# Eleven small loads at the start of a backbone block: issued from ScalarE's queue in place of SyncE's

## The chip, the cores and the metric

One core of one Trainium2 chip runs the whole program. The metric is the device time of one execution in microseconds (us). Times of a profiled execution come with a span, from its first to its last recorded work.

## The reference, cut to what matters

One layer (DEPTH is 1) of a generator block on 1024 tokens of width 1024, all in float32. The conditioning vector c gives six modulation rows; the tokens pass a multi-scale window mean with a grouped projection, a layer norm, a SwiGLU and a second layer norm.

```
s_c = silu(c);  mod_x = s_c @ mod_w + mod_b          # 1024 x 6144
sh1, sc1, g1, sh2, sc2, g2 = split(mod_x, 6)
hx = x * (1 + sc1) + sh1
p  = [window_mean(hx, w) - hx for w in (2, 4, 8, 16)]   # 256 channels each
ox = einsum('blgc,gcd->blgd', p, pool_w) * pool_scale
x  = layer_norm(ALPHA * x + g1 * ox, ln_g[0], ln_b[0])
x  = layer_norm(ALPHA * x + g2 * swiglu(x * (1 + sc2) + sh2), ln_g[1], ln_b[1])
```

## The kernel before, in words

The tokens lie in eight row tiles of 128 tokens (512 KB each), taken in two halves of four: first the tiles 1, 2, 3, 4, then 5, 6, 7, 0. The kernel first does the pooling stage, and then two long SwiGLU stages in which TensorE (PE) is nearly always busy. This case is about the first thirty microseconds.

**The modulation.** `mod_load` brings a 512 KB piece of mod_w (tile `mw`, eight pieces for each of the six modulation rows), and `mod_add` adds it on VectorE (DVE) into an accumulator `acc`, weighted by a column of `s_col`, the silu of c (line 489 for a first piece, 491 for the others). The eight pieces of sc1 come first, then those of g1. `columns` (line 506) has PE turn an accumulator into columns, and `mod_col_done` (line 518) takes them out as `sc1`.

**The window means.** For each of eight channel tiles and each token tile, `pool_inner` (line 461) multiplies the tokens by a band matrix that lies in the tile `consts` (`cst`); `pool_outer` (line 466) then adds, for a whole half, what comes from the neighbouring tokens, out of the tile `halo` (32 rows of x) and a further part of `consts` (`halo_band`). `pool_hi` (ACT, line 471) and `pool_lo` (DVE, line 474) take the result out of PSUM. `scale_bank` (PE, line 541) spreads pool_scale, which lies in `psc`, over the partitions.

**The order.** A list written out by hand, `ORDER_OF_ISSUE`, names each job in the order in which it is issued; each engine carries out its own instructions in that order. Loads are issued by SyncE (SP) in the rows shown here, one behind the other. In the list's order the first 25 loads are: 1 `rows` (c), 2 `mw`, 3 `acc` (mod_b of g1, behind a fill of `acc` by GpSimd), 4 `consts` (band matrices of two groups), 5 `mw`, 6 `x`, 7 `mw`, 8 to 10 `rows` (mod_b, ln_g, ln_b), 11 `x`, 12 `mw`, 13 `x`, 14 `mw`, 15 `x`, 16 `mw`, 17 to 20 `halo`, 21 `consts` (with `halo_band`), 22 `consts` (the other two groups), 23 and 24 `mw`, 25 `psc`. `to_columns` transposes the `rows` on PE; its first call gives `s_col` on ScalarE (ACT, line 347).

In the list, the jobs that ACT carries out are, up to the end of the first `pool_hi`: `to_columns.0` (`s_col`), and nothing else. All eleven loads that the diff touches stand ahead of that `pool_hi`: loads 4 and 8 to 10 ahead of `to_columns.0`, loads 17 to 22 and 25 behind it.

Of the kernel before, what the change touches and what calls it, by code (L numbers as in the profile page):

```python
# [17 lines left out]
P = 128  # L18
# [11 lines left out]
REACH = 8  # L30
# [189 lines left out]
def trunk_kernel(ctx: ExitStack, tc: tile.TileContext, x, c, mod_w, mod_b, ln_g, ln_b, ffn_w_in, ffn_w_out,  # L220
                 pool_w, pool_scale, consts, out):
    nc = tc.nc
# [26 lines left out]
    def big(name, dt=F32, shape=(P, 1024)):  # L249
        return take("big", name, dt, shape)  # L250
# [7 lines left out]
    def small(name, shape, bufs=1, tag=None):  # L258
        return keep.tile(list(shape), F32, tag=tag or name, name=name, bufs=bufs)
# [31 lines left out]
    tiles = {}  # L291
# [6 lines left out]
    rows = small("rows", (72, P))  # L298
# [5 lines left out]
    cst = small("consts", (P, N_MID + N_HALO + N_EDGE + N_SUMS))  # L304
# [30 lines left out]
            nc.scalar.copy(bands["starts"][:, :, at_], src)  # L335

    def vector_rows(a, b, src):
        nc.sync.dma_start(rows[a:b, :], src.rearrange("(j p) -> j p", p=P))

    def to_columns(n):  # L340

# [12 lines left out]
        nc.sync.dma_start(xr[i], x[i * P : (i + 1) * P, :])  # L354

    def load_consts(s):
        nc.sync.dma_start(cst[:, s], consts[:, s])

    def load_halo(half):
        if half == 0:  # L360
            tiles["halo",] = big("halo", F32, (32, D))
        halo, (before, after), r = tiles["halo",], HALO_ROWS[half], 2 * REACH * half
        nc.sync.dma_start(halo[r : r + REACH, :], x[before - REACH : before, :])
        nc.sync.dma_start(halo[r + REACH : r + 2 * REACH, :], x[after : after + REACH, :])

    job(fill_ones)
    job(fill_constants)
# [6 lines left out]

    def load_scale():
        tiles["psc",] = big("psc")
        nc.sync.dma_start(tiles["psc",][0:1, :], pool_scale.rearrange("(o d) -> o d", o=1))

    def mod_start(j):

# [4 lines left out]
    def gate_load(pair, kh):  # L385
        load(("wi", pair, kh), ffn_w_in[kh * HALF : (kh + 1) * HALF, pair * 256 : (pair + 1) * 256].rearrange(
            "(k p) n -> p k n", p=P), (P, 4, 256))

    job(vector_rows, 0, 8, c[0])
    job(mod_load, SC1, 0)  # L390
    job(load_consts, slice(0, 2 * BAND))
    job(mod_load, SC1, 1)
    job(load_x, ORDER[0][0])
    job(mod_load, SC1, 2)
    for a, b, src in ((8, 56, mod_b), (56, 64, ln_g[0]), (64, 72, ln_b[0])):
        job(vector_rows, a, b, src)
# [3 lines left out]
    for half in range(2):  # L400
        job(load_halo, half)
    job(load_consts, slice(N_MID, cst.shape[1]))
    job(load_consts, slice(2 * BAND, 4 * BAND))
    for k in (6, 7):
        job(mod_load, SC1, k)
    job(mod_start, G1)
    job(load_scale)
    for k in range(KT):
        job(mod_load, G1, k)
# [999 lines left out]
```

## Time and profile before

| | us |
|---|---|
| median of 3 runs | 750.62 |
| lowest, highest | 748.63, 751.89 |
| profiled execution, its own time | 749.97 |
| its span | 748.2 |

The profiled execution has 1.77 us around its span. In the rows below, PE is TensorE, PEld its weight loads, DVE VectorE, ACT ScalarE, POOL GpSimd, SP SyncE; SPq is the queue of transfers that SyncE issues. A row's "idle before <-" says how long the engine had stood still and what ended that. PEclk is the granted clock of TensorE as a share of full speed.

### The profile page before, as it was taken

The numbers are of one execution on the slowest core, as the hardware profiler recorded it, in microseconds if no ns is written. First come the engines' busy times: TensorE is split into PE (matmuls) and PEld (weight loads), VectorE is DVE, ScalarE is ACT, GpSimd is POOL, SyncE is SP. The second block draws the span as 40 slices with busy tenths as digits, with TensorE's granted clock in tenths as the row PEclk, the third lists the DMA queues.
The fourth block names the chain that finished last, engine by engine and source line by source line (L and its number), as shares of the span: only waits on it lengthen the run. The fifth ranks groups of instructions, "written<-read, shape, count | busy, mean of one in ns | idle before, by whom it ended". The sixth has DMA issues, their size and how long they took to land.

```text
span 748.2 us, 9131 instructions
## 1 busy us (share of the span) xinstructions
PE 723.9 (97%) x3326; PEld 604.8 (81%) x3326; DVE 554.9 (74%) x675; ACT 274.1 (37%) x353; POOL 168.3 (22%) x133
## 2 busy tenths in 40 slices
PE   6988999999999999999999999999999999999994
PEld 6768988888887888888888888888888888888783
DVE  3797855517288788899998777965878679646986
ACT  0321873435983221311312212212556334336411
POOL 0000000011206546483743624600000000233100
PEclk7587999999999999999999999999999999999998
DMA  8998249674929679797987798455799856999612
GB/s 303 368 409 298 114 159 375 225 237 164 330 86 292 200 239 254 210 310 241 320 264 186 240 265 212 156 202 207 277 376 391 290 193 220 262 302 286 173 57 84
DMA packets 115346, 182.85 MB, mean 244 GB/s; under 512 B 7739, under 2 KB 66819, under 8 KB 115046
## 3 DMA queue, kind: packets, MB, share of 16 engines
q1 hardware_dynamic: 108038, 164.97, 63.8%
q0 software_dynamic: 7264, 17.30, 11.5%
q8 instruction: 26, 0.43, 0.2%
q14 instruction: 18, 0.15, 0.1%
HBM read 142.14 MB, written 51.64 MB: 259 GB/s over the span
## 4 chain that ended last, share of the span: by engine, by line
PE 84%; DVE 7%; DMA 3%; ACT 3%; issue 2%; POOL 0%; SPq 0%; POOLq 0%; DVEq 0%; ACTq 0%
PE ps_v L895 39%; PE ps_x L1106 16%; PE ps_gate L761 14%; PE ps_y L1106 8%; PE ps_col L506 2%; DVE acc L491 2%; DVE ylo L270 1%; PE ps_ox L262 1%; PE ps_ox L263 1%; PE ps_ox L264 1%; DMA x<-in_x 1%; DMA consts<-in_consts 1%; ACT h L699 1%; DMA mw<-in_mod_w 1%; DVE t L270 1%
## 5 line engine op out<-in xcount | busy, mean ns | idle before, releaser
L895 PE MATMUL ps_v<-t,w0h 128*128 128x512 f32 x352 | 109.2, 391 | 0.0
L761 PE MATMUL ps_gate<-h,wih 128*128 128x512 f32 x352 | 109.0, 391 | 0.0
L267 ACT CAST yhi<-yraw 128x1024 fp32r<-128x1024 f32 x77 | 78.4, 1051 | 81.7 <-DMA yraw<-in_ffn_w_out 23.4
L270 DVE TENSOR_TENSOR ylo<-yraw,yhi 128x1024 fp32r<-128x1024 f32 x77 | 91.6, 1218 | 20.6 <-ACT yhi L267 11.4
L962 POOL TENSOR_TENSOR s<-raw,raw 128x512 f32<-128x512 f32 x22 | 31.5, 1432 | 319.3 <-DMA raw<-in_ffn_w_in 300.5
L918 ACT ACTIVATE a<-a 128x512 f32<-128x512 f32 x22 | 13.9, 632 | 229.9 <-DVE a L917 229.9
L895 PEld LDWEIGHTS ps_v<-t,w0h 128*128 128x128 f32 x352 | 66.1, 188 | 14.6 <-issue 1.0
L761 PEld LDWEIGHTS ps_gate<-h,wih 128*128 128x128 f32 x352 | 65.7, 188 | 13.7 <-issue 0.5
L491 DVE SCALAR_TENSOR_TENSOR acc<-mw,s_col,acc 128x1024 f32<-128x1024 f32 x42 | 55.9, 1331 | 19.1 <-DMA mw<-in_mod_w 18.3
L895 PE MATMUL ps_v<-t,w0l 128*128 128x512 f32 x176 | 68.6, 390 | 1.4 <-DVE w0l L270 1.4
L761 PE MATMUL ps_gate<-h,wil 128*128 128x512 f32 x176 | 68.5, 389 | 0.0
L1106 PE MATMUL ps_x<-yhi 128*128 128x512 f32 x176 | 68.5, 389 | 0.0
L1106 PE MATMUL ps_x<-ylo,yhi 128*128 128x512 f32 x176 | 68.5, 389 | 0.0
L1106 PE MATMUL ps_x<-yhi,ylo 128*128 128x512 f32 x176 | 68.5, 389 | 0.0
L895 PE MATMUL ps_v<-t,ws 128*128 128x512 f32 x264 | 63.4, 389 | 0.0
L1068 POOL DMA_DIRECT2D yraw<-in_ffn_w_out x22 | 18.7, 853 | 195.6 <-PE ps_x L1106 163.6
L895 PEld LDWEIGHTS ps_v<-t,ws 128*128 128x128 f32 x264 | 49.5, 188 | 10.3
L895 PE MATMUL ps_v<-h,w1h 128*128 128x512 f32 x176 | 54.2, 389 | 0.0
L895 PE MATMUL ps_v<-t,w1h 128*128 128x512 f32 x176 | 54.2, 389 | 0.0
L1106 PE MATMUL ps_y<-yhi 128*128 128x512 f32 x132 | 51.4, 390 | 0.9 <-DVE yv L1352 0.9
L1106 PE MATMUL ps_y<-yhi,ylo 128*128 128x512 f32 x132 | 51.4, 389 | 0.0
L1106 PE MATMUL ps_y<-ylo,yhi 128*128 128x512 f32 x132 | 51.4, 389 | 0.0
(157 smaller groups left out, 1386.5 us busy)
## 6 DMA issues: line engine op xcount, KB each, us to landing
mw<-in_mod_w SPq DMA_DIRECT2D x48, 512.0 KB, 9.2
raw<-in_ffn_w_in SPq DMA_DIRECT2D x88, 256.0 KB, 5.2
wi<-in_ffn_w_in SPq DMA_DIRECT2D x22, 512.0 KB, 6.2
yraw<-in_ffn_w_out SPq DMA_DIRECT2D x44, 256.0 KB, 5.4
yraw<-ed SPq DMA_DIRECT2D x33, 256.0 KB, 6.0
ed<-in_ffn_w_out POOLq DMA_DIRECT2D x6, 1024.0 KB, 10.5
pd<-pk SPq DMA_DIRECT2D x11, 512.0 KB, 5.2
gd<-gk SPq DMA_DIRECT2D x11, 512.0 KB, 2.9
```

The costliest lines, as they stand in the source:

```text
L262: nc.tensor.matmul(ps, lh, rh, start=first, stop=False)
L263: nc.tensor.matmul(ps, lh, rl, start=False, stop=False)
L267: nc.scalar.copy(hi, src)
L270: nc.vector.tensor_tensor(lo, src, hi.bitcast(F32), ALU.subtract)
L491: nc.vector.scalar_tensor_tensor(acc, w, s_col[:, k : k + 1], acc, ALU.mult, ALU.add)
L506: nc.tensor.matmul(tiles["ps_col", j][:, n * WIDE : (n + 1) * WIDE], t[:, n * P : (n + 1) * P], by, start=first and n == 0, stop=last and ...
L761: nc.tensor.matmul(ps, x, y, start=k == n == 0, stop=k % 4 == 3 and n == 2, skip_group_check=k > 3)
L895: nc.tensor.matmul(ps, x, y, start=fresh and first, stop=last, skip_group_check=not fresh)
L918: nc.scalar.activation(a[:, 1], a[:, 1], ACT.Silu)
L962: nc.gpsimd.tensor_tensor(s, up1, up2, ALU.add)
L1068: nc.gpsimd.dma_start(raw[n][:, 1], ADDED[n // PAIRS](n % PAIRS), accum_op=ALU.add)
L1106: nc.tensor.matmul(ps, s[x][:, r * P : (r + 1) * P], t[y][:, d], start=fresh and j == m == 0, stop=j == PAIRS - 1 and m == 2, skip_group_c ...
```

## The change

The loads of `rows` other than that of c, all three loads of `consts`, the four of `halo` and the one of `psc` are issued by ScalarE. Their place in `ORDER_OF_ISSUE`, their sizes and their destinations stay. The loads of c, `mw`, `x` and `acc` stay with SyncE.

```
     def vector_rows(a, b, src):
-        nc.sync.dma_start(rows[a:b, :], src.rearrange("(j p) -> j p", p=P))
+        (nc.sync if a == 0 else nc.scalar).dma_start(rows[a:b, :], src.rearrange("(j p) -> j p", p=P))
...
     def load_consts(s):
-        nc.sync.dma_start(cst[:, s], consts[:, s])
+        nc.scalar.dma_start(cst[:, s], consts[:, s])
...
-        nc.sync.dma_start(halo[r : r + REACH, :], x[before - REACH : before, :])
-        nc.sync.dma_start(halo[r + REACH : r + 2 * REACH, :], x[after : after + REACH, :])
+        nc.scalar.dma_start(halo[r : r + REACH, :], x[before - REACH : before, :])
+        nc.scalar.dma_start(halo[r + REACH : r + 2 * REACH, :], x[after : after + REACH, :])
...
     def load_scale():
         tiles["psc",] = big("psc")
-        nc.sync.dma_start(tiles["psc",][0:1, :], pool_scale.rearrange("(o d) -> o d", o=1))
+        nc.scalar.dma_start(tiles["psc",][0:1, :], pool_scale.rearrange("(o d) -> o d", o=1))
```

## Rows read from the trace of the kernel before

**Rows 1.** The page: the span, and the busy time of each engine.
```profile
span 748.2 us, 9131 instructions
PE 723.9 (97%) x3326; PEld 604.8 (81%) x3326; DVE 554.9 (74%) x675; ACT 274.1 (37%) x353; POOL 168.3 (22%) x133
```

**Rows 2.** The chain of work that ended last, in order of time, of its first 140 us the pieces that the text below names: start, length (us), what.
```profile
2.27 0.25 SPq L383
2.56 0.34 SPq L357
2.94 5.38 DMA mw<-in_mod_w
8.34 6.58 DMA x<-in_x
14.94 5.50 DMA consts<-in_consts
20.57 1.85 PE ps_pt L466 x8
22.43 4.44 PE ps_pt L461 x20
26.87 1.91 PE ps_psc L541 x4
28.78 2.73 PE ps_col L506 x16
...
32.21 1.28 DVE acc L491
...
40.23 3.52 PE ps_g L548 x4
...
95.44 38.11 PE ps_gate L761 x168
```

**Rows 3.** The queue of SP in order of time: start, time of the issue (us), line, transfer.
```profile
4.36 0.61 SPq L338 DMA_DIRECT2D rows<-in_mod_b  x1
5.02 0.93 SPq L338 DMA_DIRECT2D rows<-in_ln_g  x1
5.99 0.36 SPq L338 DMA_DIRECT2D rows<-in_ln_b  x1
6.39 0.35 SPq L354 DMA_DIRECT2D x<-in_x  x1
...
8.34 0.33 SPq L354 DMA_DIRECT2D x<-in_x  x1
...
11.03 0.33 SPq L354 DMA_DIRECT2D x<-in_x  x1
...
14.94 1.75 SPq L357 DMA_DIRECT2D consts<-in_consts  x2
17.65 2.13 SPq L295 DMA_DIRECT2D mw<-in_mod_w  x2
19.82 0.29 SPq L377 DMA_DIRECT2D psc<-in_pool_scale  x1
```

**Rows 4.** What SP's queue waited for in the first 30 us: us in total, times, longest.
```profile
SPq L354 <- DMA mw<-in_mod_w: 2.9, 3, 1.1
SPq L357 <- DMA x<-in_x: 1.0, 1, 1.0
```

**Rows 5.** PE, DVE and ACT in order of time up to 32 us: start, us, engine, line, operation, operands, and in brackets the idle time before and what ended it.
```profile
17.68 2.08 PE L461 MATMUL ps_pt<-consts,x 128*128 128x129 f32 x8 [0.61 <-DMA x<-in_x]
20.57 1.85 PE L466 MATMUL ps_pt<-consts,halo 32*128 32x16 f32 x8 [0.81 <-DMA consts<-in_consts]
...
8.42 1.28 DVE L491 SCALAR_TENSOR_TENSOR acc<-mw,s_col,acc 128x1024 f32<-128x1024 f32 x1 [0.77 <-DMA mw<-in_mod_w]
11.11 1.28 DVE L491 SCALAR_TENSOR_TENSOR acc<-mw,s_col,acc 128x1024 f32<-128x1024 f32 x1 [1.41 <-DMA mw<-in_mod_w]
27.24 1.28 DVE L491 SCALAR_TENSOR_TENSOR acc<-mw,s_col,acc 128x1024 f32<-128x1024 f32 x1 [0.18 <-DMA mw<-in_mod_w]
31.53 0.17 DVE L518 SCALAR_TENSOR_TENSOR sc<-ps_col,cols 128x8 f32<-128x8 f32 x1 [3.01 <-PE ps_col L506]
...
0.74 1.28 ACT L347 ACT_TABLE_LOAD   x1 [0.74 <-PEq L1396]
6.65 0.21 ACT L347 ACTIVATE s_col<-cols 128x8 f32<-128x8 f32 x1 [4.63 <-DVE cols L345]
21.18 2.06 ACT L471 CAST pt<-ps_pt 128x512 fp32r<-128x512 f32 x4 [14.32 <-PE ps_pt L466]
```

**Rows 6.** Stretches of the start (A:B in us): length, busy time of each engine with its instructions, then the granted clock of TensorE, the share of the 16 DMA engines that was busy, and what they moved in GB/s.
```profile
core 0: us, PE busy (x) PEld busy (x) DVE busy (x) ACT busy (x) POOL busy (x), PEclk, DMA share, GB/s
4.00:6.00 2.00, 2.00 (x12) 2.00 (x11) 0.00 (x0) 0.00 (x0) 0.00 (x0) 1.00 0.77 213
10.00:18.00 8.00, 6.54 (x26) 5.71 (x27) 3.98 (x4) 0.00 (x0) 0.00 (x0) 0.50 1.02 401
22.40:26.20 3.80, 3.80 (x18) 3.80 (x18) 3.51 (x5) 2.08 (x6) 0.00 (x0) 0.50 1.00 364
26.50:29.50 3.00, 3.00 (x15) 1.62 (x14) 1.84 (x2) 1.17 (x2) 0.00 (x0) 1.00 1.02 407
29.80:31.50 1.70, 1.70 (x10) 1.70 (x10) 0.00 (x0) 0.00 (x0) 0.00 (x0) 0.50 0.99 395
```

**Rows 7.** Transfers by issuing line in the first 35 us: engine, count, size of one, median us from issue to landing.
```profile
halo<-in_x SPq DMA_DIRECT2D x4, 32.0 KB
consts<-in_consts SPq DMA_DIRECT2D x2, 144.0 KB, 4.4
consts<-in_consts SPq DMA_DIRECT2D x1, 100.0 KB, 5.5
```

**Rows 8.** Waits between 20 and 100 us, that of the accumulations for their loads: us in total, times, longest.
```profile
DVE acc L491 <- DMA mw<-in_mod_w: 2.0, 2, 1.8
```

## The prediction

> **What bounds the kernel now.** The page comes first: PE is busy for 97% of the span [rows 1]. From 95 us on the chain of work is PE at its dense SwiGLU matmuls [rows 2], so a change in the loads of the first 20 us can only move the moment at which that stretch begins. The next view is therefore the chain in order of time. Its start is three transfers in a row: a piece of mod_w (2.94, 5.38 us), a tile of x (8.34, 6.58 us), and a load of `consts` (14.94, 5.50 us), which lets PE begin `pool_outer` at 20.57 [rows 2]. From there PE runs without a break to 31.5, DVE waits for it (the accumulations from 32.21 on), and so on to the dense stretch [rows 2].
>
> Why each transfer of that chain begins as the one before lands is seen in SP's queue. The issue at 8.34 is load 13, and it waits for load 5; the issue at 14.94 is load 21, and it waits for load 13 [rows 3, 4]. So a load is held until the one eight places ahead of it in the list has landed. It is not the time of an issue (0.3 to 0.9 us [rows 3]) that spaces the later loads, but this rule and the rate of the DMA engines, which between 10 and 18 us are full: share 1.02, 401 GB/s [rows 6]. Only before that is there room: 0.77 and 213 GB/s from 4 to 6 us [rows 6].
>
> **The change part by part.** I assume that the rule of eight places goes on counting over both queues; the trace has one hardware queue only, and the last rival takes the other case.
>
> *Loads 4 and 8 to 10 leave SP.* Load 5 (`mw`) follows load 3, whose issue starts at 2.27 behind GpSimd's fill, so it can be issued at 2.56 in place of 2.94: 0.38 us earlier [rows 2]. Load 11 (`x`), issued at 6.39, no longer stands behind the three issues from 4.36 on, 2.0 us [rows 3]. What this is worth is bounded by the gap in the rate: from 4 to 6 us (401 - 213) GB/s x 2 us = 0.38 MB are not moved, which is 0.94 us at 401 GB/s. Below, it is worth nothing, if the DMA engines and not the queue made the gap: 1.5 MB (loads 5 to 7) had been issued by then and still ran at 213 GB/s. I take 0.38 us, the shift of load 5, as that load alone is on the chain.
>
> *Loads 17 to 21 go to ACT's queue.* Load 21 still waits for load 13, so it is issued no earlier than that lands, about 14.5. But in SP's queue it took 5.5 us for 100 KB [rows 7], behind the 512 KB loads issued ahead of it; on a queue of its own it has none ahead. The trace has no small load on a second queue: bounds are nothing saved (5.5 us), and the 100 KB at 401 GB/s, 0.26 us, besides a start that no row gives. The nearest small load in a shorter queue is one of the two 144 KB `consts`, whose median is 4.4 us [rows 7]. Even at 4.4 us it would land at 19.0 and be off the path, since the next thing late is PE itself: the eight matmuls of the fourth x tile run from 17.68 for 2.08 us, to 19.76 [rows 5]. So the most that the earlier `consts` alone gives is PE's wait, 0.81 us [rows 5].
>
> The Trainium skill, DMA: Bandwidth & Descriptors, section "Issuing engines are not separate DMA queues", says that loads from different engines end on the same 16 DMA engines, and that issuing from several saves only the issuing time; by that sentence `consts` lands no sooner and the sum would be nothing. Its section "Queues, rings and completion order" says that each DMA engine takes turns between the queues that have work; by that one `consts` passes the big loads. No row of before can choose, as it has one such queue.
>
> *What the small loads take from the big ones.* If they pass, the fourth x tile (load 15, issued at 11.03, landing at 17.65) has four `halo` loads and one `consts` ahead of it that used to be behind: 4 x 32 + 100 = 228 KB [rows 7], 0.58 us at 401 GB/s. With load 22 (144 KB) too it is 0.95 us; if they don't pass, nothing. I take 0.58, since load 22 is held until load 14 has landed, shortly ahead of load 15.
>
> *ACT's side.* Eleven issues at 0.29 to 0.93 us each [rows 3] are some 4 to 5 us of ACT's queue. ACT has a table load to 2.02, `s_col` at 6.65, and then stands idle for 14.32 us until 21.18 [rows 5]: that idle time covers the seven issues behind `s_col`. The last two wait for loads 14 and 17, long landed by the 17.65 and 19.82 at which SP went on [rows 3]. Ahead of `s_col` stand four issues; the last of them is load 10, held until load 2 has landed, which was so by 5.99 [rows 3]. With its own 0.36 us that is 6.35, before 6.65. Should ACT's table load stand behind it, `s_col` ends near 7.8 and the first accumulation near 8.6 in place of 8.42; the next one waits 1.41 us for its load anyway [rows 5]. So ACT's side is put at nothing; without that idle time the 4 to 5 us would fall on `pool_hi` one for one.
>
> *Sum.* The fourth x tile lands 0.38 us earlier and 0.58 us later, so PE is through with it at 19.76 + 0.20 = 19.96 and begins `pool_outer` there and not at 20.57: 0.6 us earlier. From there the gain passes on: PE 20.57 to 31.5 without a break, then DVE, which had waited 3.01 us for it [rows 5] and so could gain that much, and later accumulations find their loads there: after 20 us their waits sum to 2.0 us in two pieces, and those lie ahead of 28 us [rows 5, 8]. Bounds: best 0.94 earlier and nothing taken, `pool_outer` at 18.82, a gain of 1.75; worst nothing earlier and 0.95 taken, at 20.71, a loss of 0.14.
>
> So 749.97 - 0.6 = 749.4 for the profiled execution. That execution lies 0.65 under the median of three, 750.62; for the median I say 750.0.
>
> **The rivals.**
>
> *Hidden anyway (0.18).* `consts` lands as late as before, or what the small loads take eats the gain. For it: the DMA engines are full from 10 us on [rows 6], and no byte is saved. Against: only 0.81 us of a 5.5 us landing must go. Time: 750.6. The sentence of the skill named first above would end here.
>
> *The clock rises sooner (0.12).* PE's granted clock is 0.50 (1.2 GHz) in 22.40 to 26.20 and 1.00 (2.4 GHz) in 26.50 to 29.50 [rows 6]; it rose after PE had run without a break from 20.57. Without the 0.81 us gap the unbroken run begins at 17.68, and the rise may come by 22.4. Then 3.8 us of matmuls take half, 1.9 us, and with 0.6 the gain is 2.5, within DVE's 3.01: 748.1. Against: the long gap of that row is not the only one, and I cannot tell when a rise comes.
>
> *Slower: ACT's queue is held at its head (0.07).* If the issues on ACT run late, `pool_hi` waits behind the load of `psc`. It decides once that issue ends after 21.18; each us beyond goes into `pool_hi`, the PSUM banks and the `pool_lo` on DVE behind it. Past 0.5% needs that issue at 25 us, over 5 us later than SP's 19.82 [rows 3]: 754.5 or more. Against: the 14.32 us of idle.
>
> *The clock's fast stretch is lost (0.06).* If PE's start shifts so that the stretch 26.50 to 29.50 stays at 0.50, its 3 us cost 6: 750.0 + 3.0 = 753.0, on the slow side, within 0.5%.
>
> *Eight places for each queue, and the gap of the start filled (0.05).* SP's big loads then run further ahead, the small ones are free of waits: the bound of 1.75 with the clock's 1.9, 3.7 us: 747.0.
>
> *The forecast (0.52):* 750.0, with a range of its own from 749.0 to 750.8.
>
> **How the numbers follow.** About 0.5%, 3.75 us, is what a measurement of this kernel can tell from no change. None of the cases but the held queue, and the edge of the last, passes it. Faster by more: 0.08 (the last case, and half of a clock that also stays up later); slower by more: 0.08 (the held queue, with a little of the lost stretch); the rest 0.84. The runs shown spread from 748.63 to 751.89 by themselves. The range takes in the earlier clock below and most of the lost stretch above: 747.2 to 752.6.
>
> **What would show it.** In the profile of the changed kernel: `consts` and `halo` on a second queue, the 100 KB load landing within 4 us; SP's second `mw` issue near 2.56; the wait of `pool_outer` for `consts` gone, its start between 19.8 and 20.2, right behind the fourth x tile's matmuls; `s_col` under 8 us; the first `pool_hi` 0.6 us after `pool_outer`; line 518 on DVE near 31. The prediction is wrong if `pool_outer` still waits for `consts`, if x tiles land over a microsecond later, if `pool_hi` starts behind an issue, or if the granted clock between 20 and 32 us, or between 60 and 80, is not that of before.

## The result: 0.44% slower, and where the time went

The changed kernel has a median of 753.53 us over 22 runs (750.81 to 756.17), the kernel before 750.14 over 22 runs beside it (748.21 to 753.96): a ratio of 1.0044, 95% interval 1.003 to 1.0057. That is 3.4 us slower, just under the 0.5% at which the prediction drew its line, on the other side of the forecast 750.0 and outside the range of 747.2 to 752.6.

The chain that ended last, of the changed kernel, in order of time (start, length in us, what):
```profile
1.06 5.49 PE ps_warm L321 x24
6.54 0.22 PE ps_cols L344
7.31 0.51 ACTq L364
7.86 5.89 DMA halo<-in_x
13.77 0.34 SPq L354
14.15 0.43 SPq L295
14.62 7.07 DMA x<-in_x
21.74 2.09 PE ps_pt L461 x8
23.83 1.82 PE ps_pt L466 x8
25.64 4.87 PE ps_pt L461 x20
30.51 2.15 PE ps_psc L541 x4
32.66 2.02 PE ps_col L506 x16
...
35.38 1.28 DVE acc L491
```
Before, the chain ran through a piece of mod_w, a tile of x and a load of `consts` to `pool_outer` at 20.57 [rows 2]. Now it runs through the warm-up matmuls at the start (line 321), the transpose of c (line 344) and an issue on ScalarE's queue (ACTq) to a load of `halo`, and `pool_outer` (line 466) begins at 23.76, 3.19 us later; VectorE's accumulations begin at 35.38 and not at 32.21.

SyncE's queue of the changed kernel (start, time of the issue, line, transfer):
```profile
3.01 0.33 SPq L295 DMA_DIRECT2D mw<-in_mod_w  x1
4.96 0.33 SPq L354 DMA_DIRECT2D x<-in_x  x1
5.33 0.43 SPq L295 DMA_DIRECT2D mw<-in_mod_w  x1
5.80 0.43 SPq L354 DMA_DIRECT2D x<-in_x  x1
13.30 0.33 SPq L295 DMA_DIRECT2D mw<-in_mod_w  x1
13.77 0.34 SPq L354 DMA_DIRECT2D x<-in_x  x1
```
and what that queue waited for in the first 40 us (us in total, times, longest):
```profile
SPq L295 <- DMA halo<-in_x: 7.1, 1, 7.1
...
SPq L354 <- DMA rows<-in_mod_b: 1.6, 1, 1.6
```
From 6.23 to 13.30 SyncE issues nothing: its sixth big load, load 12 of the list, waits 7.1 us for a load of `halo`. Before, load 12 was issued at 6.79, right behind load 11's 6.39 [rows 3]. ScalarE in order of time, its queue and its work, shows why that `halo` load is so late:
```profile
2.24 0.28 ACTq L338 DMA_DIRECT2D rows<-in_ln_b  x1
2.56 1.28 ACT L347 ACT_TABLE_LOAD   x1 [2.56 <-issue]
6.98 0.21 ACT L347 ACTIVATE s_col<-cols 128x8 f32<-128x8 f32 x1 [3.14 <-DVE cols L345]
6.99 0.28 ACTq L363 DMA_DIRECT2D halo<-in_x  x1
7.31 0.51 ACTq L364 DMA_DIRECT2D halo<-in_x  x1
```
The `halo` loads stand behind `s_col`, which waits for its columns until 6.98. Issued then, the second one lands at about 13.3, behind the big loads already in flight. Meanwhile those finish, and the DMA engines run dry (stretch, length, busy time of PE, PEld, DVE, ACT, POOL, then granted clock of TensorE, busy share of the DMA engines, GB/s):
```profile
10.00:14.00 4.00, 2.12 (x10) 1.84 (x10) 1.42 (x2) 0.00 (x0) 0.00 (x0) 0.56 0.45 161
...
10.00:18.00 8.00, 4.21 (x17) 3.63 (x17) 1.58 (x3) 0.00 (x0) 0.00 (x0) 0.53 0.70 237
```
From 10 to 18 us they moved 401 GB/s before [rows 6] and 237 now: 164 GB/s x 8 us = 1.31 MB, which at 401 GB/s is 3.3 us, near the 3.19 us of `pool_outer`. That it comes so near is in part the choice of the stretch: over the first 20 us the mean fell from 303 to 250 GB/s, which by the same sum is 2.6 us.

**Which load waits for which.** The program as built gives every transfer of SyncE and ScalarE one of eight semaphores (counters that tell of a landing), in turn, and a transfer waits until the one that had its semaphore before has landed. That is the rule of eight places that the prediction read from the trace. But the turn does not follow the list once there are two queues: it goes back and forth between them, so that ScalarE's loads, few and near the head of their queue, come up early. In the numbers of the list (A for ScalarE, S for SyncE), eight to a line:
```
4A   1S   8A   2S   9A   10A  3S   17A
5S   18A  6S   19A  7S   20A  11S  21A
22A  12S  25A  13S  14S  15S  16S  23S
```
A load waits for the one above it: load 12 for the `halo` load 18, load 13 for 19, load 15 for 20; load 6 for load 8, the `rows` of mod_b in the wait above. The first and the last of these waits are the ones that the trace shows, 7.1 and 1.6 us. In the kernel before, load 12 stood behind load 4, which had long landed.

### The profile page after: what moved, and what is told of

Same layout as the page of the kernel before. It is cut to its first block, busy times and chain, and to the rows that moved or that the text cites. A ratio compares the mean times of both kernels' runs of the same rounds, so it can differ in the third digit from the quotient of the medians.

```text
span 749.9 us, 9129 instructions
## 1 busy us (share of the span) xinstructions
PE 721.9 (96%) x3326; PEld 602.3 (80%) x3326; DVE 566.1 (75%) x675; ACT 273.8 (37%) x353; POOL 170.0 (23%) x133
## 4 chain that ended last, share of the span: by engine, by line
PE 85%; DVE 6%; DMA 3%; issue 2%; ACT 2%; POOL 0%; SPq 0%; POOLq 0%; ACTq 0%; DVEq 0%
PE ps_v L895 38%; PE ps_x L1106 16%; PE ps_gate L761 14%; PE ps_y L1106 9%; DVE acc L491 2%; PE ps_col L506 2%; PE ps_pt L461 2%; DMA yraw<-a2d 1%; DMA x<-in_x 1%; DVE ylo L270 1%; PE ps_ox L262 1%; PE ps_ox L264 1%; PE ps_ox L263 1%; DMA halo<-in_x 1%; PE ps_warm L321 1%
## 5 line engine op out<-in xcount | busy, mean ns | idle before, releaser
L491 DVE SCALAR_TENSOR_TENSOR acc<-mw,s_col,acc 128x1024 f32<-128x1024 f32 x42 | 53.7, 1281 | 21.8 <-DMA mw<-in_mod_w 21.2
```

The lines of the kernel that those rows point to most:

```text
L491: nc.vector.scalar_tensor_tensor(acc, w, s_col[:, k : k + 1], acc, ALU.mult, ALU.add)
```

## The experiments

Theory A: SyncE is held by a small load that has an early turn but is issued late, behind `s_col`; the loss is the time for which the DMA engines then have nothing to do. Theory B: the early small loads slow the big ones on the DMA engines. Theory C: ScalarE as an issuer costs by itself. All times are medians with the kernel before beside them on the same chip; the ratio and its interval are worked out from all the runs and can differ by 0.1% from the quotient of the two medians; "pool_outer" is its start in the profiled execution.

| kernel | pool_outer, us | median | before | ratio, 95% interval |
|---|---|---|---|---|
| before | 20.57 | | | |
| changed | 23.76 | 753.53 | 750.14 | 1.0044 (1.003 to 1.0057) |
| e1 start alone | 19.24 | 749.10 | 749.42 | 0.9996 (0.9977 to 1.0014) |
| e2 all but halo | 24.75 | 754.65 | 749.42 | 1.0077 (1.0058 to 1.0097) |
| e3 halo alone | 23.73 | 753.15 | 749.42 | 1.0053 (1.0033 to 1.0073) |
| e4 halo by GpSimd | 23.08 | 753.20 | 749.42 | 1.0059 (1.0038 to 1.008) |
| e5 before, held to 12.5 | 23.30 | 751.90 | 749.27 | 1.0029 (1.001 to 1.0048) |
| e6 changed, 1 warm-up | 20.78 | 750.42 | 749.27 | 1.0011 (0.9995 to 1.0027) |
| e7 before, 1 warm-up | 20.35 | 749.09 | 749.27 | 0.9994 (0.9975 to 1.0013) |
| e8 start ScalarE, late GpSimd | 20.35 | 748.00 | 749.27 | 0.9981 (0.996 to 1.0003) |
| e9 before, held to 10 | 21.47 | 750.17 | 750.01 | 0.9998 (0.9981 to 1.0014) |
| e10 late GpSimd | 20.96 | 749.85 | 750.01 | 0.999 (0.9967 to 1.0012) |
| e11 as e8 | 20.46 | 749.21 | 750.01 | 0.9988 (0.9973 to 1.0003) |

**e1: only the loads ahead of `s_col` on ScalarE.** Against the changed kernel:
```
-        nc.scalar.dma_start(cst[:, s], consts[:, s])
+        (nc.scalar if s.start == 0 else nc.sync).dma_start(cst[:, s], consts[:, s])
...
(halo and psc: nc.sync again)
```


> Only the rows loads and the first consts load (those ahead of s_col) go to ScalarE; halo, the other consts and psc are SyncE's again. Theory A (slots: a load is held until the one eight places ahead in the dealing order has landed, the dealing alternates between the two queues, and in the changed kernel SyncE's big loads are therefore held by halo loads): nothing late stands in a slot ahead of a big load, SyncE issues x and mw up to the fourth x tile by 8 us, the DMA engines stay full from 6 to 18 us, pool_outer starts at 19.5 to 20.5, time 749.3 to 750.2 against 750.1 of before. Theory B (traffic: the early halo loads slow the big loads on the DMA engines themselves): no halo is early here, so 749.3 to 750.2 too. Theory C (ScalarE as an issuer costs, by s_col or a second queue): 751.5 to 753.5.

The loss is gone. SyncE's second piece of mod_w goes out at 2.55 and the fourth x tile at 7.14 (11.03 before [rows 3]), the DMA engines stay at 1.02 from 10 to 14 us, and `pool_outer` starts at 19.24, 1.33 us sooner than before and a little ahead of the expected 19.5 to 20.5. Of SyncE's queue the fourth x tile, and PE's row:
```profile
7.14 0.45 SPq L354 DMA_DIRECT2D x<-in_x  x1
```
```profile
19.24 1.85 PE L466 MATMUL ps_pt<-consts,halo 32*128 32x16 f32 x8 [0.67 <-DMA consts<-in_consts]
```
So issuing from ScalarE does not cost as such: theory C had 751.5 or more. But the median does not follow those 1.33 us. In the profiled execution they were lost at once. A stretch of e1, columns as above, and then VectorE's row of `sc`:
```profile
26.50:29.50 3.00, 3.00 (x4) 0.66 (x2) 1.61 (x2) 0.58 (x1) 0.00 (x0) 0.50 1.03 416
```
```profile
33.31 0.17 DVE L518 SCALAR_TENSOR_TENSOR sc<-ps_col,cols 128x8 f32<-128x8 f32 x1 [5.16 <-PE ps_col L506]
```
The granted clock stayed at 0.50 (1.2 GHz) in the stretch that had 1.00 (2.4 GHz) before [rows 6], and `sc` came at 33.31 and not at 31.53. That is the rival of the lost fast stretch, seen in one execution, and one of the slower ones of e1 (751.40, of 12 runs from 747.87 to 751.51); whether it is so in most of them no run shows.

**e2: all but `halo` on ScalarE, and e3: `halo` alone.**
```
e2   halo: nc.sync again; the rest as changed
e3   halo: nc.scalar; rows, consts, psc: nc.sync again
```


> The change without its halo part: rows, all consts and psc on ScalarE, halo on SyncE. Theory A: the third x tile now stands eight places behind a consts load that ScalarE issues after s_col (about 7 us); SyncE is held until that lands, some 10 to 11 us in place of 13.3, with five big loads in flight and not four; a short dry stretch of the DMA engines; 750.3 to 752. Theory B: the halo loads are late again, so 749.3 to 750.2. Theory C: 752.5 to 753.5.

> Only the four halo loads go to ScalarE. They are then its first instructions, issued from 0.7 us on, and land before SyncE's loads behind them in the same slots are due. Theory A: no hold on a halo load beyond 6 us, the DMA engines full from 7 to 18 us, 749.5 to 750.7. Theory B: the same 128 KB even earlier, beside the first mw pieces, 752 to 754. Theory C: 751.5 to 753.5.

Both are slower, e2 by more than the change itself, and both expectations of theory A were too low: taken alone, e3 lies in the ranges of B and C, and e2 above all three. For e3 mine had a plain mistake: the `halo` loads are not ScalarE's first instructions, since `s_col` stands ahead of them in the list. In e3, of ScalarE in order of time, and of SyncE's waits the longest (there it is load 8, `rows` of mod_b, that is held, and all behind it):
```profile
6.29 0.58 ACTq L363 DMA_DIRECT2D halo<-in_x  x1
```
```profile
SPq L338 <- DMA halo<-in_x: 6.3, 1, 6.3
```
In e2, of SyncE's waits the longest, and then a piece of the chain that ended last:
```profile
SPq L354 <- DMA consts<-in_consts: 5.9, 1, 5.9
```
```profile
7.26 7.12 DMA consts<-in_consts
```
So a load of `halo` or of `consts` will do, if it has an early turn and stands behind `s_col`. In e2 more comes to it. From 10 to 18 us the engines moved 278 GB/s, by the sum above 2.5 us, less than in the change; but the `halo` loads, SyncE's again, go out from 15.72 on, and `pool_outer` waits for them behind the fourth x tile:
```profile
24.75 1.86 PE L466 MATMUL ps_pt<-consts,halo 32*128 32x16 f32 x8 [1.30 <-DMA halo<-in_x]
```
So the dry stretch is not the whole of e2's delay of 4.18 us.

What I had mis-sized is the landing of the small load: I took 3 to 4 us, and it was 5.5 to 7.1. In e2 the first of these `consts` was issued at 6.87, behind four of SyncE's big loads (2.55 to 6.60) and ahead of the fifth (7.07); x of 6.60 let PE go on at 12.56, and `consts` let SyncE go on at 13.39. Loads of the two queues land, as far as this shows, about in the order in which they were issued.

**e4: the changed kernel with `halo` on GpSimd's queue.**
```
-        nc.scalar.dma_start(halo[...
+        nc.gpsimd.dma_start(halo[...
```


> The changed kernel, but with the four halo loads issued by GpSimd, whose transfers take slots of their own. Theory A: the halo loads no longer hold SyncE; what is left is the hold of the third x tile by a consts load as in the run without the halo part, 750.3 to 752. Theory B: the halo traffic is as early as in the changed kernel or earlier, 752.5 to 754. Theory C: 752.5 to 753.5.

It lies in the range of B and C, above that of A. But SyncE's long wait is again there, on `consts`, as in e2 (of its waits the longest):
```profile
SPq L354 <- DMA consts<-in_consts: 6.4, 1, 6.4
```
and so it doesn't tell the theories apart. e5 and e8 do.

**e5 and e9: SyncE held, with no second queue.** The kernel before; load 12 waits for a one-column fill of its tile on VectorE, and the loads behind it keep their order (lines from 295 on are three higher).
```
+        if key == ("mw", SC1, 3):
+            nc.vector.memset(t[:, 0:1], 0.0)
         nc.sync.dma_start(t, src)
...
(order: mod_load.3 and the loads behind it after mod_add.2; in e9 after mod_add.1)
```


> The kernel before, all loads on SyncE, but its load 12 (mw) is made to wait for a one-column fill of its tile that VectorE carries out behind the third accumulation; SyncE so stands still from about 6.5 to 12.5 us, as long as it does in the changed kernel, with the same four big loads in flight. No second queue, no early small load. Theory A (the standing still of SyncE, by whatever wait, lets the DMA engines run dry and is the whole loss): the engines fall under 0.5 busy between 11 and 13 us, pool_outer starts at 22.8 to 24, time 2.5 to 4 us over before, 752 to 753.5. Theory B (the early small loads cost) and theory C (the second queue costs): no more than 1 us over before.

> As the run that holds SyncE to 12.5 us, but its load 12 waits for VectorE's second accumulation and not the third: SyncE goes on near 10 us, with about two big loads still in flight. Theory A: the engines hardly run dry, pool_outer starts at 20.6 to 21.8, 0 to 1.2 us over before; together with the longer hold this gives the loss as a function of the hold alone.

Held to 12.80, SyncE leaves the engines as dry as the change does, and `pool_outer` starts at 23.30. A stretch of e5, then PE's row:
```profile
10.00:14.00 4.00, 3.42 (x14) 3.15 (x15) 1.63 (x4) 0.00 (x0) 0.00 (x0) 0.50 0.38 120
```
```profile
23.30 1.86 PE L469 MATMUL ps_pt<-consts,halo 32*128 32x16 f32 x8
```
The loss is 0.29% (0.1 to 0.48) for a `pool_outer` 2.73 us later: A's cause alone, without early small loads and without ScalarE, makes a loss of this kind. It is 2.2 us by the ratio and 2.6 by the medians, a little less than the change's 3.4 and at the low end of what was expected; the two intervals overlap, and whether the rest has a cause of its own is open. In e9, held to 10.46, the engines stay at 0.88 from 10 to 14 us. The stretch of e9, then PE's row:
```profile
10.00:14.00 4.00, 3.17 (x13) 2.89 (x14) 1.84 (x4) 0.00 (x0) 0.00 (x0) 0.50 0.88 272
```
```profile
21.47 1.85 PE L469 MATMUL ps_pt<-consts,halo 32*128 32x16 f32 x8 [0.46 <-DMA consts<-in_consts]
```
`pool_outer` is still 0.90 us late, but the median doesn't move by more than its interval, some 1.2 us either way. So of SyncE's wait the part up to 10.5 us, with loads still in flight, cost little or nothing that the runs can tell, and the part behind it, when they had run out, is what was paid.

**e6 and e7: the same change with `s_col` sooner.**
```
-WARM = 12
+WARM = 1
```


> The changed kernel with 1 warm-up matmul in place of 12, so that the transpose behind the warm-up, s_col, and with it the issue of the halo loads behind s_col on ScalarE come about 3 us sooner (near 4 in place of 6.99). No load is moved. Theory A, with the order on ScalarE's queue as the cause of the late halo loads: the halo loads are issued near 4 us, land by 8 to 10, SyncE goes on then and not at 13.3, pool_outer starts at 20 to 21.5, time 0 to 1.5 us over the kernel before with 1 warm-up matmul. Theory B and C: the distance to that kernel stays at 3 to 3.5 us.

> The kernel before with 1 warm-up matmul: the control for the run above. All theories: its loads keep their times, the first 20 us are paced by transfers; within 1 us of before, 749.4 to 751, unless the granted clock of the start matters.

With one warm-up matmul PE transposes c sooner. The columns that `s_col` waits for are there by 2.95, so that ScalarE's queue goes on to `halo` at 2.99, while `s_col` itself runs at 3.84, behind the load of its table. In e6, of ScalarE in order of time the first `halo` load, of SyncE's waits those for `halo`, and of PE `pool_outer`, then that of e7:
```profile
2.99 0.31 ACTq L363 DMA_DIRECT2D halo<-in_x  x1
```
```profile
SPq L354 <- DMA halo<-in_x: 2.3, 1, 2.3
...
SPq L295 <- DMA halo<-in_x: 1.2, 1, 1.2
```
```profile
20.78 1.06 PE L466 MATMUL ps_pt<-consts,halo 32*128 32x16 f32 x8
```
```profile
20.35 1.76 PE L466 MATMUL ps_pt<-consts,halo 32*128 32x16 f32 x8 [1.06 <-DMA consts<-in_consts]
```
The turns are the same and no load was moved, yet the wait of 7.1 us has become two of 1.2 and 2.3, `pool_outer` is 0.43 us later than in e7 and not 3.19, and the distance to its own control has shrunk from 3.4 to 1.3 us (750.42 against 749.09). So it is the place behind a late `s_col` that makes the turns expensive. How much of the median is due to that alone is less sure: in the two profiled executions the granted clock differs as well (from 20 to 24 us it was 1.00 in e6 and 0.56 in e7).

**e8, e10 and e11: the late small loads on GpSimd, whose transfers take turns of their own.**
```
rows, first consts   e8, e11: nc.scalar   e10: nc.sync
halo, other consts, psc               nc.gpsimd
```


> Rows and the first consts load on ScalarE as in the change, but halo, the other consts and psc on GpSimd, which has slots of its own; SyncE issues big loads alone. All the small loads are as early as in the changed kernel or earlier. Theory A: no hold of SyncE beyond the pace of its own loads, the engines full from 7 to 18 us, pool_outer at 18.8 to 20, 748.5 to 750. Theory B: the early traffic costs, 752 to 754. Theory C: as the changed kernel's start alone, no loss seen there, so 749 to 750.

> Halo, the last two consts and psc on GpSimd; rows and the first consts load stay with SyncE, nothing goes to ScalarE. Theory A: no hold of SyncE by a small load; pool_outer at 19.8 to 20.8, 748 to 750. If the gain of the run with the start on ScalarE and the late ones on GpSimd (748.0) comes from the late ones alone, this is the same within 0.7 us; if it comes from the start, it stands at before.

> The version with rows and the first consts load on ScalarE and the late small loads on GpSimd, timed once more, as its interval touched 1: if it is faster, 747.5 to 749 and an interval below 1; if not, 749 to 750.

All small loads of e8 are as early as in the change or earlier, and no small load holds SyncE for more than 1.0 us (`rows` of mod_b). The transfers of e8 in the first 35 us (transfer, engine, count, size, median us to landing), and PE's row of `pool_outer`:
```profile
consts<-in_consts ACTq DMA_DIRECT2D x1, 144.0 KB, 2.2
consts<-in_consts POOLq DMA_DIRECT2D x1, 144.0 KB, 7.5
halo<-in_x POOLq DMA_DIRECT2D x4, 32.0 KB, 6.2
consts<-in_consts POOLq DMA_DIRECT2D x1, 100.0 KB, 7.2
```
```profile
20.35 1.89 PE L466 MATMUL ps_pt<-consts,halo 32*128 32x16 f32 x8
```
`pool_outer` starts a little behind the expected 18.8 to 20. The time is that of before or a little less: 0.9981 and 0.9988, both intervals reaching just past 1. Theory B falls: the traffic is there and no loss. That e8 beats both kernels is likely and not shown; it clearly beats the changed one. e10 stands at 0.999, between; whether the start or the late loads would bring that microsecond is open.

## Why the prediction was wrong

**The step that failed** is the sentence "I assume that the rule of eight places goes on counting over both queues", in the way I used it: in the order of the list. The rule itself held. The order in which it counts did not, and with it fell the forecast that SyncE's loads would only move earlier, or later by what the small ones carry. A hold of SyncE by a load on ScalarE's queue is no term of the sum and is in none of the rivals, so it stood at nothing. The runs show it in the place of the gain of 0.6 us: a wait of 7.1 us, `pool_outer` 3.19 us later, 3.4 us in the median. The same order is why the prediction had load 10 wait till about 6 us; it went out at 2.24. I asked what ScalarE's queue does to the work behind it there (does it hold `pool_hi`?) and not what a load late on ScalarE's queue does to SyncE.

**The second failing step** is "on a queue of its own it has none ahead". The 100 KB load of `consts` took 5.5 us behind SyncE's big loads before [rows 7]; behind some of them it took 6.5 and 6.9 us on ScalarE's queue (e2, e4) and 7.2 on GpSimd's (e8), and 144 KB took 2.2 us where nothing was ahead (e8). The small loads didn't pass. Of the two sections of the Trainium skill that the prediction weighed (DMA: Bandwidth & Descriptors), "Issuing engines are not separate DMA queues" is the one that the landings agree with; the taking of turns of the other gave the small loads no such lead in these runs.

**The term "what the small loads take from the big ones"**, 0.58 us, was not what decided: in e8, where they go early and hold nothing, and in e1, where the four first ones do, `pool_outer` is 0.2 and 1.3 us sooner, inside the bounds of -0.14 to +1.75.

**What held.** The 0.81 us wait of `pool_outer` for `consts` is gone: it follows the fourth x tile's matmuls at once. The 100 KB load did land within 4 us: issued at 12.83, it let load 23, which waits for it, go out at 15.99. But not for the reason given: by then the engines had run nearly empty. `s_col` ran at 6.98, under 8 us; `pool_hi` came 0.64 us after `pool_outer`; ScalarE's own idle time did cover its issues, so the held-queue rival, as written, did not happen. SyncE's second piece of mod_w came at 3.01 and not 2.56, as its turn stood behind the first `consts`; in e1, where it doesn't, it came at 2.55. And a delay at `pool_outer` passes to the end about one for one, within the 1.5 us or so that the intervals leave: 3.19 us there and 3.4 in the median for the change, 4.18 and 5.2 in e2, 3.16 and 3.7 in e3, 2.51 and 3.8 in e4, 2.73 and 2.6 in e5. Of the prediction's own signs of being wrong one came at once: the fourth x tile landed at about 21.7, and not at 17.65.

**The clock.** The profiled execution of the changed kernel is only 1.7 us longer in span than that of before, though `pool_outer` is 3.19 later. The difference lies between 66 and 78 us; of the changed kernel, then of the kernel before:
```profile
66.00:70.00 4.00, 3.35 (x24) 3.35 (x24) 3.96 (x5) 1.04 (x1) 0.00 (x0) 0.81 1.09 348
```
```profile
66.00:70.00 4.00, 4.00 (x20) 4.00 (x20) 2.24 (x2) 1.04 (x1) 0.00 (x0) 0.50 1.09 348
```
There the changed kernel was granted 0.81 in place of 0.50. Its dense stretch begins at 97.00 against 95.44 [rows 2], so about half of the 3.19 us came back in this one execution. The medians, over 22 runs each, keep the 3.4. The fast stretch of the start was neither lost nor sooner in this execution: the clock was 1.00 from 32 to 34 us, where before it was 1.00 from 26.5 to 29.5 [rows 6].

## What to carry to other kernels

A transfer moved to another engine's queue takes that engine's program order with it, and where both queues draw on the same few completion semaphores, a load stuck there behind a compute instruction holds the other queue too (7.1 us here). Before moving small loads, read for each big load which transfer's landing it waits for after the move, and when that transfer can be issued. Here small loads on a second queue landed behind the big ones already in flight, so moving them saved issue time alone: 1.33 us at `pool_outer` in e1, and nothing in its median that the runs can tell.

## What the runs showed of the hardware that was not expected

- Small loads on a second or third queue did not overtake the big ones: 100 KB issued behind at least four 512 KB loads, not all of which had landed, took 6.5 and 6.9 us on ScalarE's queue (e2, e4) and 7.2 on GpSimd's (e8), against 5.5 on SyncE's own before; 144 KB with nothing ahead took 2.2 us.
- An earlier start of TensorE's work can be lost to its granted clock, as one execution of e1 shows: 1.33 us gained at `pool_outer`, and 1.78 us late at `sc`, 14 us further on, at 0.50 in place of 1.00.
- A stop of the issuing queue cost only once its loads had run out: stopped from 6.23 to 13.30 the engines were 0.45 busy from 10 to 14 us and 3.4 us were lost; stopped to 10.46 (e9) they were 0.88 busy and no loss shows.
